# A bank for each product of a small expert, units split at most two ahead, the tail's reloads ahead of the last gate unit, and another order of its additions

## The chip, the cores and the metric

The kernel runs on one core of one Trainium2 chip. The metric is the device time of one execution in microseconds (us), the median of three runs. TensorE is called PE, ScalarE ACT, VectorE DVE, GpSimd POOL; SP issues most of the transfers (DMA).

## The reference, cut to what matters

One decoder layer over 1024 tokens of width 1024: a mixer, a mixture of 32 experts of which each token uses two, a gated addition of a per-layer input embedding (PLE), and a final norm.

```python
def expert_block(args):                      # for each expert, its rows xb
    xb, e = args
    hmid = jax.nn.silu(xb @ w1[e]) * (xb @ w3[e])
    return hmid @ w2[e]
...
h = h + hier_moe(...)                        # gates times the two experts' rows, added
e = rms_norm(p[l] @ w_ple_up[l], ple_norm[l])
gate = jax.nn.sigmoid(rms_norm(h, ple_gate_norm[l]) @ w_ple_gate[l])
h = h + gate * e
return rms_norm(h, final_norm)
```

## The kernel before

**Experts.** After routing, the experts are sorted by their number of tokens. The schedule of 32 places is `HHHHLHLHLHLHLLHLHLHLHLLHLHLHLHLL`: H is a heavy expert (up to 128 rows), L a light one (up to 64 rows; `self.light[e]`), places counted from 0. Two lights stand together at places 12 and 13, 21 and 22, and 30 and 31. Each expert has six weight units of 1 MB, two each for `w1`, `w3`, `w2`. A unit's raw copy lies in a slot (`raw`, `rawB`, `rawH`, `hb`; 13 slots in turn, so a unit's transfer waits until the unit 13 before it has let its slot go). From place 26 (`EP`) on only the six slots of `raw` and `rawB` are used. A light expert's matmuls read the raw slot itself (`W.plain`), which is free when PE has read it. A heavy expert's unit is **split** first: ACT writes the high part (L160, into `wh` or `XH`, in turn), DVE the low part (L162); the slot is free when both have read it. Each 128x512 product of a heavy expert is three matmuls (high by high, low by high, high by low; L248 to L250).

**Order.** Instructions run on each engine in the order in which this code writes them. For place `e` the loop of `moe` writes: `gemm1(e, 1)` into bank `a`; the transposes of `h` of `e-1` and their copies (`hth`, or `ht` for a light one); Silu on ACT (L1588); `gemm1(e, 3)`; the product on DVE (L1590); the transposes of the next expert's rows and their copy (`xth`, or `xt`); `gemm2(e-1)` with its result `y` and the scatter to `Y_dram`. Units are asked for in the order w1(e), w3(e), w2(e-1).

**Looking ahead.** `W.get(u, look)` writes the splits of unit `u` and of the next `look` units of heavy experts, passing over those of light ones, ahead of `u`'s matmuls:

```python
        while n < len(self.units) and (n in self.plain or look):
            look -= n not in self.plain
            n += 1
```

A split that is written early stands early in ACT's order, and what is written after it waits behind it for the unit's transfer.

**Banks.** A light expert's two products share one PSUM tile `acc`: columns 0 to 255 hold x·w1, 256 to 511 x·w3. Waits are made per tile.

**Tail.** The PLE products run as a generator (`ple`, L1201 to L1224) in half tiles of six matmuls; `fill(n)` runs n of them. `load(t)` reads tile t's two expert rows back from `Y_dram`, `tail_load(t)` the residual, `add(t)` adds them (four additions on DVE, L1798), `trans(t)` transposes the sum (L1807) and splits it into `gth`, `gtl`, `first(t)` is the first half of the gate's product, `finish` the sigmoid and what follows. There are four gate units of 1 MB.

Of the kernel before, what the change touches and what calls it, by code (L numbers as in the profile page):

```python
# [10 lines left out]
F32 = mybir.dt.float32  # L11
# [3 lines left out]
AF = mybir.ActivationFunctionType  # L15
OP = mybir.AluOpType
# [6 lines left out]
P = 128  # L23
# [12 lines left out]
NSTATIC, NLIGHT = 3, 16  # L36
HB = P // 2
# [172 lines left out]
class Layer:  # L210
# [1233 lines left out]
    def gather(self, e):  # L1444

        r, n = self.rank[e], HB if self.light[e] else P
        self.nc.gpsimd.indirect_dma_start(
            out=self.xg[e % 2][:n], out_offset=None, in_=self.g_dram,
            in_offset=bass.IndirectOffsetOnAxis(ap=self.idx_g[:n, r:r + 1], axis=0),
            bounds_check=T - 1, oob_is_err=False)  # L1450


    def moe(self):
        tc, nc, W = self.tc, self.nc, self.W
        psA, psB = self.psA, self.psB
# [7 lines left out]
        XT, HT, RX = {}, {}, {}  # L1463

        def norm_x(e):
            x = xg[e % 2]
            RX[e] = ep.tile([P, 1], F32, name="rx", bufs=3)
            if self.light[e]:
                for b in range(2):
                    nc.gpsimd.tensor_copy(RX[e][b * HB:b * HB + HB], x[:HB, D:D + 1])  # L1470
            else:
                nc.gpsimd.tensor_copy(RX[e], x[:, D:D + 1])
# [24 lines left out]
        def gemm1(e, which, acc):  # L1497
            for ui, u in enumerate(self.eu[e, which]):
                w = W.get(u, self.look(e, which))
                for kk in range(4):  # L1500
                    k = ui * 4 + kk
                    if self.light[e]:

                        o = (which == 3) * 256
                        for b in range(2):
                            self.lastmm = nc.tensor.matmul(acc[b * HB:b * HB + HB, o:o + 256], XT[e][:, k],  # L1506
                                                           w[:, kk, b * 256:b * 256 + 256],
                                                           start=k == 0, stop=k == KD - 1)
                    else:
                        th, tl = XT[e]  # L1510
                        self.mm3(acc, th[:, k], tl[:, k], w[0][:, kk], w[1][:, kk], k == 0, k == KD - 1)
                if self.light[e]:
                    W.done(u)
# [48 lines left out]
        for e in range(NE + 1):  # L1562
            last = e == NE
            if e == self.EP:
                W.split_to(self.ple_unit)
                self.ple_open()
            if not last:
                light = self.light[e]
                a = psA.tile([P, 512], F32, name="acc")
                b = a if light else psA.tile([P, 512], F32, name="acc")  # L1570
                if e + 2 < NE:
                    gather(e + 2)
                if e + 1 < NE:
                    norm_x(e + 1)
                if not e:
                    next(order)
                gemm1(e, 1, a)
                if not e:
                    next(order)
                    W.limit = 1 << 30  # L1580
            if e and e - 1 in hs:
                trans_h(e - 1, hs.pop(e - 1))
            if not last:
                h = ep.tile([P, 512], F32, name="h")
                a0 = a
                if light:
                    h, a, b = h[:, :256], a[:, :256], a[:, 256:]
                nc.scalar.activation(h, a, AF.Silu, scale=RX[e])  # L1588
                gemm1(e, 3, a0 if light else b)
                nc.vector.scalar_tensor_tensor(h, b, RX.pop(e), h, op0=OP.mult, op1=OP.mult)  # L1590
                hs[e] = h
                if not e:
                    next(order, None)
                if e + 1 < NE:
                    trans_x(e + 1)
            if e:
                gemm2(e - 1, (lambda: trans_h(e, hs.pop(e))) if e + 1 == NE else None)
                self.mark("moe %d" % (e - 1))
            if e >= 2:
                next(blocks, None)  # L1600
            if e > self.EP and not last:
                next(self.ple_gen)
# [3 lines left out]
    def look(self, e, which):  # L1606
        if which == 2 and e == NE - 1:
            return 0
        return 3


    def overflow_list(self):
# [157 lines left out]
    def tail(self):  # L1770
        tc, nc, i, W = self.tc, self.nc, self.i, self.W
        psA, psB = self.psA, self.psB
# [4 lines left out]
        def load(t):  # L1777
            if t % 2:
                y = self.rawB_pool.tile([P, 2048], F32, name="rawB", bufs=3)
            else:  # L1780
                y = self.ring.tile([P, 2048], F32, name="raw", bufs=3)
            ty[t] = (y[:, :D], y[:, D:])
            if t:
                nc.sync.dma_start(ty[t][0], self.Y_dram[t * P:(t + 1) * P])
                nc.sync.dma_start(ty[t][1], self.Y_dram[T + t * P:T + (t + 1) * P])
            else:
                for c in range(2):
                    s = slice(c * 512, c * 512 + 512)
                    nc.sync.dma_start(y.rearrange("p (k d) -> p k d", k=2)[:, :, s],  # L1789
                                      self.Y_dram.rearrange("(k t) d -> t k d", k=2)[:P, :, s])  # L1790

        def add(t):
            h = self.th[t]
            y0, y1 = ty[t]
            for c in range(2):
                for y in (y0, y1):
                    s = slice(c * 512, c * 512 + 512)
                    v.tensor_tensor(h[:, s], h[:, s], y[:, s], op=OP.add)  # L1798

        def trans(t):  # L1800
            h = self.th[t]
            th = tq.tile([P, KD, P], F32R, name="gth")
            tl = tq.tile([P, KD, P], F32R, name="gtl")
            for b in range(2):
                p = psB.tile([P, 4, P], F32, name="pb")
                for k in range(4):
                    nc.tensor.transpose(p[:, k, :], h[:, (4 * b + k) * P:(4 * b + k + 1) * P], self.ident)  # L1807
                self.split_pair(th[:, 4 * b:4 * b + 4], tl[:, 4 * b:4 * b + 4], p)
            gt[t] = (th, tl)
            st = rs[t] = tq.tile([P, 2], F32, name="tst")  # L1810
            nc.scalar.activation(ty[t][1], h, AF.Square, accum_out=st[:, 0:1])  # L1811
            self.rstd(st[:, 1:2], st[:, 0:1], D)
# [45 lines left out]
        def fill(n):  # L1858
            for _ in range(n):
                next(self.ple_gen, None)  # L1860


        W.end = None
        W.fetch_to(len(W.units))
        self.tail_load(1)
        load(0)
        load(1)
        fill(2)
        W.split_to(self.gate_units[0] + 1)
        fill(2)  # L1870
        W.split_to(self.gate_units[1] + 1)
        fill(3)
        add(0)
        fill(1)
        add(1)
        fill(1)
        self.ctxE.close()
        tq = ctxQ.enter_context(tc.tile_pool(name="tq", bufs=2, side="right", reuse_waits="tile"))
        self.fn = self.tp.tile([P, D], F32, name="tpt")
        trans(0)  # L1880
        sg = tq.tile([P, 1], F32, name="sg", bufs=1)
        nc.scalar.activation(sg, self.ones[:, 0:1], AF.Sigmoid)  # L1882
        fill(1)
        trans(1)
        fill(3)
        self.tail_load(2)
        load(2)
        nc.sync.dma_start(self.fn, bcast_rows(i["final_norm"], D))
# [3 lines left out]
        def first(t, mid=None):  # L1892
            acc = accs[t] = psA.tile([P, 512], F32, name="acc")
            gemm(t, 0, acc, mid=mid)
            finish(t, 0, acc)
# [12 lines left out]
        for t in range(NT):  # L1908
            acc = [None, None]
            if not t:  # L1910
                W.split_to(self.gate_units[2] + 1)
                first(0)
                W.ahead = 99
                W.split_to(len(W.units))
                first(1)
                add(2)
            elif t > 1:
                first(t)
            if t:
                following(t)  # L1920
            acc[1] = psA.tile([P, 512], F32, name="acc")
            if t < NT - 1:
                gemm(t, 1, acc[1])
                finish(t, 1, acc[1])
            else:
                for a, s in ((acc[1], slice(0, 256)), (psA.tile([P, 512], F32, name="acc"), slice(256, 512))):
                    gemm(t, 1, a, s)
                    finish(t, 1, a, s)
            self.mark("gate %d" % t)
            if 2 < t + 2 < NT:  # L1930
                add(t + 2)
# [52 lines left out]
```

## Time and profile before

| what | us |
|---|---|
| median of 3 runs (1308.75 to 1311.0) | 1310.31 |
| the profiled execution's own time | 1312.78 |
| its span, first to last instruction | 1311.1 |
| PE busy | 1197.2 (91%) |
| ACT busy | 581.3 (44%) |
| DVE busy | 706.3 (54%) |

Times in the trace are us from the start of the span. The experts run from about 590 to 1172, the tail from there on. "Idle before, releaser" in brackets is how long an engine stood before a row and which instruction ended that. A busy PE can run at either of two clocks; the granted clock is 1.00 at the upper one and 0.50 at the lower.

### The profile page before, as it was taken

What the parts mean: (1) busy time and instruction counts of PE and PEld (TensorE: products, weight loads), DVE (VectorE), ACT (ScalarE), POOL (GpSimd) and SP (SyncE); (2) the same over time, 40 slices, a digit from 0 to 9 for tenths busy, and PEclk for the clock granted to TensorE, in tenths of its full rate; (3) what the DMA queues carried; (4) which work ended last, traced back from release to release, by engine and by line L of the source; (5) the groups of instructions that cost most, each with busy time, mean ns of one, the idle gap of its engine ahead of it and who ended that gap; (6) DMA issues with size and microseconds to landing.
All of it is one profiled execution on the core that took longest, in us unless ns stands there. A gap on an engine that the chain in (4) does not pass through costs nothing. (4 is left out here: it accounts for less than half of the span.)

```text
span 1311.1 us, 17704 instructions
## 1 busy us (share of the span) xinstructions
PE 1197.2 (91%) x6559; PEld 932.6 (71%) x6559; DVE 706.3 (54%) x1128; ACT 581.3 (44%) x931; POOL 270.5 (21%) x378
## 2 busy tenths in 40 slices
PE   7999999999999999969999985998959987886997
PEld 7987888988888888757876663666635655544886
DVE  3557745437763545869964443454423535226665
ACT  5744343444443334227764443454423535234442
POOL 1043112305211433121211110111102101111232
PEclk9999999999999999979999997999979987898999
DMA  9323331322324356957989998999979889666421
GB/s 346 137 96 112 105 128 58 113 97 97 121 89 177 118 209 240 370 184 300 370 338 398 410 394 351 383 409 407 394 303 403 324 316 364 223 246 240 168 90 64
DMA packets 60094, 317.80 MB, mean 242 GB/s; under 512 B 9708, under 2 KB 10284, under 8 KB 30436
## 3 DMA queue, kind: packets, MB, share of 16 engines
q1 hardware_dynamic: 48196, 284.76, 56.5%
q0 software_dynamic: 11664, 31.83, 6.9%
q8 instruction: 53, 0.87, 0.3%
q14 instruction: 37, 0.30, 0.1%
q10 hardware_dynamic: 144, 0.04, 0.0%
HBM read 295.59 MB, written 29.46 MB: 248 GB/s over the span
## 5 line engine op out<-in xcount | busy, mean ns | idle before, releaser
L248 PE MATMUL acc<-wh,XH 128*128 128x512 f32 (+2 forms) x544 | 210.3, 387 | 7.6 <-ACT wh L160 6.7
L249 PE MATMUL acc<-wl,XH 128*128 128x512 f32 (+2 forms) x544 | 202.5, 372 | 1.1 <-DVE wl L162 1.1
L250 PE MATMUL acc<-wh,XL 128*128 128x512 f32 (+2 forms) x544 | 203.1, 373 | 0.3 <-DVE XL L379 0.3
L162 DVE TENSOR_TENSOR wl<-raw,wh 128x2048 fp32r<-128x2048 f32 (+4 forms) x62 | 102.7, 1672 | 82.1 <-ACT wh L160 81.8
L248 PEld LDWEIGHTS acc<-wh,XH 128*128 128x128 f32 x544 | 104.0, 191 | 23.3 <-ACT wh L160 6.9
L250 PEld LDWEIGHTS acc<-wh,XL 128*128 128x128 f32 x544 | 103.8, 191 | 17.1 <-DVE XL L379 0.5
L249 PEld LDWEIGHTS acc<-wl,XH 128*128 128x128 f32 x544 | 103.9, 191 | 16.0 <-DVE wl L162 1.6
L160 ACT ACTIVATE wh<-raw 128x2048 fp32r<-128x2048 f32 (+4 forms) x62 | 86.5, 1414 | 49.3 <-PE acc L250 28.7
L1548 POOL DMA_INDIRECT Y_dram<-y,idx_s x16 | 16.3, 1020 | 251.5 <-ACT y L1547 251.5
L1506 PE MATMUL acc<-rawH,xt 128*64 128x256 f32 x288 | 37.3, 413 | 33.5 <-ACT h L1588 30.5
L1541 POOL DMA_INDIRECT Y_dram<-y,idx_l x16 | 17.0, 1062 | 217.1 <-ACT y L1540 196.6
L162 DVE TENSOR_TENSOR XL<-raw,XH 128x1024 fp32r<-128x1024 f32 x30 | 35.3, 1219 | 48.6 <-ACT XH L160 48.6
L1590 DVE SCALAR_TENSOR_TENSOR h<-acc,rx,h 128x512 f32<-128x512 f32 (+1 forms) x32 | 19.6, 614 | 76.5 <-PE acc L1506 65.4
L1506 PEld LDWEIGHTS acc<-rawH,xt 128*64 128x64 f32 x288 | 21.6, 149 | 49.3 <-ACT h L1588 31.4
L248 PE MATMUL acc<-XH,xth 128*128 128x512 f32 x128 | 53.9, 421 | 0.3 <-ACT xth L266 0.3
L250 PE MATMUL acc<-XH,xtl 128*128 128x512 f32 x128 | 51.4, 402 | 0.3 <-DVE xtl L267 0.3
L1506 PE MATMUL acc<-raw,xt 128*64 128x256 f32 x208 | 30.3, 442 | 23.3 <-ACT h L1588 21.2
L249 PE MATMUL acc<-XL,xth 128*128 128x512 f32 x128 | 51.4, 402 | 0.0
L248 PE MATMUL acc<-XH,wh 128*128 128x512 f32 x128 | 50.9, 398 | 0.0
L248 PE MATMUL acc<-wh,xth 128*128 128x512 f32 x128 | 50.7, 396 | 0.0
L249 PE MATMUL acc<-XL,wh 128*128 128x512 f32 x128 | 50.6, 396 | 0.0
L250 PE MATMUL acc<-XH,wl 128*128 128x512 f32 x128 | 50.6, 395 | 0.0
(475 smaller groups left out, 2816.5 us busy)
## 6 DMA issues: line engine op xcount, KB each, us to landing
rawB<-in_w SPq DMA_DIRECT2D x56, 1024.0 KB, 9.9
raw<-in_w SPq DMA_DIRECT2D x53, 1024.0 KB, 11.2
rawH<-in_w SPq DMA_DIRECT2D x48, 1024.0 KB, 14.2
hb<-in_w SPq DMA_DIRECT2D x34, 1024.0 KB, 12.7
raw<-in_w_in SPq DMA_DIRECT2D x24, 1024.0 KB, 4.9
raw<-in_w_out SPq DMA_DIRECT2D x8, 1024.0 KB, 4.9
raw<-in_w_in SPq DMA_DIRECT2D x8, 768.0 KB, 6.5
xl<-in_x SPq DMA_DIRECT2D x4, 1024.0 KB, 9.5
```

The lines of the kernel that those rows point to most:

```text
L160: self.nc.scalar.activation(h[:, s], r[:, s], AF.Copy)
L162: low.tensor_tensor(l[:, s], r[:, s], h[:, s].bitcast(F32), op=OP.subtract)
L248: self.lastmm = mm(out, lh, rh, start=first, stop=False)
L249: mm(out, lh, rl, start=False, stop=False)
L250: mm(out, ll, rh, start=False, stop=last)
L1506: self.lastmm = nc.tensor.matmul(acc[b * HB:b * HB + HB, o:o + 256], XT[e][:, k], w[:, kk, b * 256:b * 256 + 256], start=k == 0, stop=k == ...
L1541: st = nc.gpsimd.indirect_dma_start(out=self.Y_dram.rearrange("t (c d) -> (t c) d", c=2), out_offset=bass.IndirectOffsetOnAxis(ap=self.idx ...
L1548: st = nc.gpsimd.indirect_dma_start(out=self.Y_dram, out_offset=bass.IndirectOffsetOnAxis(ap=self.idx_s[:, r:r + 1], axis=0), in_=y, in_of ...
L1590: nc.vector.scalar_tensor_tensor(h, b, RX.pop(e), h, op0=OP.mult, op1=OP.mult)
```

## The change

It does five things. A light expert's products get a bank each (`b` is always a tile of its own). `look` falls from 3 to 2 from place 3 on. In the tail, the rows of tiles 0 and 1 are asked for ahead of the last gate unit. The load of the sigmoid's table is written at the start of the tail. And `add(0)`, `add(1)`, `trans(1)` and the split of the third gate unit are written later among the PLE's halves: `trans(1)` now stands between the two units of `first(0)`.

```diff
-                        o = (which == 3) * 256
                         for b in range(2):
-                            self.lastmm = nc.tensor.matmul(acc[b * HB:b * HB + HB, o:o + 256], XT[e][:, k],
+                            self.lastmm = nc.tensor.matmul(acc[b * HB:b * HB + HB, :256], XT[e][:, k],
...
-                b = a if light else psA.tile([P, 512], F32, name="acc")
+                b = psA.tile([P, 512], F32, name="acc")
...
-        return 3
+        return 3 if e < NSTATIC else 2
...
+        load(0)
+        self.tail_load(1)
+        load(1)
         W.end = None
         W.fetch_to(len(W.units))
-        self.tail_load(1)
-        load(0)
-        load(1)
+        nc.scalar.activation(self.pst[:, 0:1], self.ones[:, 0:1], AF.Sigmoid)
         fill(2)
         W.split_to(self.gate_units[0] + 1)
         fill(2)
         W.split_to(self.gate_units[1] + 1)
-        fill(3)
+        fill(4)
         add(0)
-        fill(1)
-        add(1)
-        fill(1)
+        fill(2)
...
         trans(0)
-        sg = tq.tile([P, 1], F32, name="sg", bufs=1)
-        nc.scalar.activation(sg, self.ones[:, 0:1], AF.Sigmoid)
         fill(1)
-        trans(1)
-        fill(3)
+        add(1)
+        fill(2)
...
-                W.split_to(self.gate_units[2] + 1)
-                first(0)
+                first(0, lambda: trans(1))
```

On PE, the light expert at place 12 (rows of x in `xt`; its w1 product, the transposes of the heavy expert's `h`, its w3 product), before:

```order
L1506 MATMUL acc<-rawH,xt_6625 64x256 [waits DMAHW2_49,Activation_49]
L1506 MATMUL acc<-rawH,xt_6625 64x256 x7
L1506 MATMUL acc<-raw,xt_6625 64x256 [waits DMAHW3_49]
L1506 MATMUL acc<-raw,xt_6625 64x256 x7
L1729 MATMUL pb<-cst,h 128x128 [waits DVE_49]
L1729 MATMUL pb<-cst,h 128x128 x3
L1506 MATMUL acc<-rawH,xt_6625 64x256 [waits DMAHW4_49,Activation_49]
L1506 MATMUL acc<-rawH,xt_6625 64x256 x7
```

And now:

```order
L1505 MATMUL acc<-rawH,xt_6629 64x256 [waits DMAHW2_49,Activation_49]
L1505 MATMUL acc<-rawH,xt_6629 64x256 x7
L1505 MATMUL acc<-raw,xt_6629 64x256 [waits DMAHW3_49]
L1505 MATMUL acc<-raw,xt_6629 64x256 x7
L1726 MATMUL pb<-cst,h 128x128 [waits DVE_49]
L1726 MATMUL pb<-cst,h 128x128 x3
L1505 MATMUL acc<-rawH,xt_6629 64x256 [waits DMAHW4_49]
L1505 MATMUL acc<-rawH,xt_6629 64x256 x7
```

The order is the same; the first matmul of the w3 product no longer waits for ACT. The wait that is left at the first row is for the copy `xt`.

On ACT, the same place (the `y` of the light expert before, the heavy expert's `hth`, the light one's Silu into `h`, the rows `xt` of place 13, and the first two units of the heavy expert at place 14, `XH<-rawB` and `wh<-rawH`), before:

```order
L1483 ACTIVATE xt_6625<-pb 128x512
L1540 ACTIVATE y<-pb,gate_l 128x512
L160 ACTIVATE XH<-rawB 128x1024 x2
L266 ACTIVATE hth<-pb 128x512
L1588 ACTIVATE h<-acc,rx 128x256
L1483 ACTIVATE xt_6739<-pb 128x512
L160 ACTIVATE wh<-rawH 128x1024 x2
```

And now:

```order
L1483 ACTIVATE xt_6629<-pb 128x512
L1539 ACTIVATE y<-pb,gate_l 128x512
L266 ACTIVATE hth<-pb 128x512
L1585 ACTIVATE h<-acc,rx 128x256
L1483 ACTIVATE xt_6740<-pb 128x512
L160 ACTIVATE XH<-rawB 128x1024 x2
L160 ACTIVATE wh<-rawH 128x1024 x2
```

The split `XH<-rawB` moved behind `hth`, the Silu and `xt`. Every split of a heavy expert's unit from place 3 on moves back in this way by the work of one unit.

On SP, the first transfers of the tail (`xt` and `rawH` are residual tiles, `raw` and `rawB` rows of `Y_dram` or the last gate unit), before:

```order
L1768 DMA xt<-h_dram 128x1024
L120 DMA raw<-in_w_ple_gate 128x2048
L1768 DMA xt<-h_dram 128x1024
L1789 DMA raw<-Y_dram 128x2x512 x2
L1784 DMA rawB<-Y_dram 128x1024
L1785 DMA rawB<-Y_dram 128x1024
```

And now:

```order
L1765 DMA xt<-h_dram 128x1024
L1786 DMA raw<-Y_dram 128x2x512 x2
L1765 DMA xt<-h_dram 128x1024
L1781 DMA rawB<-Y_dram 128x1024
L1782 DMA rawB<-Y_dram 128x1024
L120 DMA raw<-in_w_ple_gate 128x2048
```

Tile 0's rows now stand ahead of 1.5 MB that stood before them, and the gate unit is last. SP's order among the experts is as it was.

## Rows read from the trace of the kernel before

**Rows 1.** The page's 40 slices of the span: busy share of the DMA engines, tenths.

```profile
DMA  9323331322324356957989998999979889666421
```

**Rows 2.** Windows: us, busy PE, PEld, DVE, ACT, POOL; granted clock, DMA share, GB/s.

```profile
650.00:670.00 20.00, 18.95 (x123) 13.33 (x122) 12.14 (x18) 10.53 (x14) 2.18 (x3) 1.00 0.77 297
670.00:800.00 130.00, 119.32 (x674) 81.86 (x673) 67.09 (x75) 64.41 (x84) 21.77 (x29) 0.99 1.01 403
800.00:830.00 30.00, 18.80 (x126) 12.38 (x128) 8.37 (x9) 9.26 (x13) 2.16 (x3) 0.77 0.81 318
830.00:960.00 130.00, 116.95 (x674) 78.35 (x670) 61.91 (x65) 60.25 (x79) 20.83 (x29) 0.99 1.01 404
960.00:980.00 20.00, 10.10 (x54) 6.62 (x55) 4.92 (x6) 5.91 (x8) 0.00 (x0) 0.62 0.60 233
1030.00:1110.00 80.00, 66.22 (x351) 43.54 (x350) 36.16 (x38) 35.02 (x47) 12.02 (x17) 0.88 0.86 329
1110.00:1172.00 62.00, 53.40 (x299) 32.37 (x297) 14.93 (x21) 17.97 (x34) 7.42 (x11) 0.93 0.64 233
```

**Rows 3.** Timeline of PE: start, us, line, operation, count, idle before and releaser.

```profile
729.43 1.95 PE L1506 MATMUL acc<-rawH,xt 128*64 128x256 f32 x16 [1.10 <-ACT h L1588]
...
810.47 5.81 PE L1506 MATMUL acc<-rawH,xt 128*64 128x256 f32 x32 [13.24 <-ACT h L1588]
...
969.90 3.68 PE L1506 MATMUL acc<-rawH,xt 128*64 128x256 f32 x16 [15.02 <-ACT h L1588]
...
1053.22 3.68 PE L1506 MATMUL acc<-raw,xt 128*64 128x256 f32 x16 [6.01 <-ACT h L1588]
...
1093.14 3.68 PE L1506 MATMUL acc<-raw,xt 128*64 128x256 f32 x16 [7.74 <-ACT h L1588]
...
1137.11 3.68 PE L1506 MATMUL acc<-raw,xt 128*64 128x256 f32 x16 [4.52 <-ACT h L1588]
```

**Rows 4.** Timeline of ACT around the wait at 810.

```profile
807.57 2.00 ACT L160 ACTIVATE XH<-rawB 128x1024 fp32r<-128x1024 f32 x2 [13.58 <-DMA rawB<-in_w]
809.48 0.58 ACT L266 ACTIVATE hth<-pb 128x512 fp32r<-128x512 f32 x1
```

**Rows 5.** Timeline of ACT: two splits of equal place in neighbouring pairs.

```profile
909.95 2.00 ACT L160 ACTIVATE XH<-rawB 128x1024 fp32r<-128x1024 f32 x2 [8.06 <-DMA rawB<-in_w]
...
944.98 2.00 ACT L160 ACTIVATE XH<-raw 128x1024 fp32r<-128x1024 f32 x2 [8.42 <-DMA raw<-in_w]
```

**Rows 6.** Timeline of PE and ACT before the wait at 1093, and ACT before that at 1053.

```profile
1081.19 3.62 PE L1506 MATMUL acc<-rawB,xt 128*64 128x256 f32 x32
...
1084.50 2.00 ACT L160 ACTIVATE XH<-raw 128x1024 fp32r<-128x1024 f32 x2 [6.09 <-DMA raw<-in_w]
...
1090.23 2.00 ACT L160 ACTIVATE XH<-rawB 128x1024 fp32r<-128x1024 f32 x2 [0.46 <-DMA rawB<-in_w]
...
1050.32 2.00 ACT L160 ACTIVATE XH<-rawB 128x1024 fp32r<-128x1024 f32 x2 [6.61 <-DMA rawB<-in_w]
```

**Rows 7.** Timeline of the tail's start: SP, PE, DVE and ACT.

```profile
1180.68 0.98 SPq L1789 DMA_DIRECT2D raw<-Y_dram x2
...
1184.69 1.40 DVE L1201 SCALAR_TENSOR_TENSOR rawH<-acc,pst,pn 128x512 f32<-128x512 f32 x2
...
1186.80 0.40 PE L248 MATMUL acc<-rawHh,tps 128*128 128x512 f32 x1
...
1187.97 0.40 PE L250 MATMUL acc<-rawHh,tps 128*128 128x512 f32 x1
...
1188.87 2.75 DVE L1798 TENSOR_TENSOR xt<-xt,raw 128x512 f32<-128x512 f32 x4 [2.78 <-DMA raw<-Y_dram]
...
1192.72 2.02 DVE L1798 TENSOR_TENSOR xt<-xt,rawB 128x512 f32<-128x512 f32 x3 [0.50 <-DMA rawB<-Y_dram]
...
1201.09 1.28 ACT L1882 ACT_TABLE_LOAD   x1
...
1205.77 0.76 PE L248 MATMUL acc<-XH,gth 128*128 128x512 f32 x1 [6.86 <-ACT pjunk L1222]
```

More of the change, by code (lines that the diff above doesn't have):

```diff
@@ L1584, in moe @@
                 h = ep.tile([P, 512], F32, name="h")
[L1585 to L1590, printed above, removed]
+                n = 256 if light else 512
+                nc.scalar.activation(h[:, :n], a[:, :n], AF.Silu, scale=RX[e])
+                gemm1(e, 3, b)
+                nc.vector.scalar_tensor_tensor(h[:, :n], b[:, :n], RX.pop(e), h[:, :n], op0=OP.mult, op1=OP.mult)
                 hs[e] = h
```

## The prediction

> **What bounds the kernel now.** I began with the page's slices of the span. There the DMA engines are nearly full from slice 18 on, where the experts run [rows 1], so I cut that stretch into windows. For 130 us from 670 and for 130 us from 830 their share is 1.01 at 403 and 404 GB/s [rows 2]. A pair of a heavy and a light expert (12 units of 1 MB, with gathers and scatters) costs the transfers about 35 us: the same split in neighbouring pairs waits for its DMA until 909.95 and 944.98, 35.0 us apart [rows 5]. PE needs less for the pair. In the two long windows it is busy 119.3 and 117.0 of 130 us and loses little [rows 2]. So in this stage the transfers set the pace, and a wait of PE costs time only where it makes the DMA engines stand.
>
> They do stand. The timeline of PE shows five long waits for the Silu of a light expert, 13.24, 15.02, 6.01, 7.74 and 4.52 us, and a usual one of 1.10 [rows 3]. The timeline of ACT shows why: at 807.57 a split of a unit of a later heavy expert has waited 13.58 us for its transfer, and `hth` and the Silu stand behind it in ACT's order [rows 4]. PE holds the light units' slots meanwhile. So when the late unit has landed, the transfers have filled all 13 slots and wait for PE: share 0.81 in 800 to 830, 0.60 in 960 to 980 [rows 2]. PE's clock also falls in such a wait and comes back some us later (0.77 and 0.62 there). From 1030 on only six slots serve and the share is 0.86, then 0.64 [rows 2].
>
> In the tail, the timeline shows DVE waiting for tile 0's rows until 1188.87, then for tile 1's, and PE waiting 6.86 us until the first gate matmul at 1205.77 [rows 7]. From there PE runs on to the end almost without a wait, so what that matmul gains, the kernel gains.
>
> **The change, part by part**, against the profiled execution's own 1312.8 us.
>
> *Bank and look, experts to 1030.* The bank takes away the usual 1.10 us of each light expert, but in a stage that the transfers bound this pays nothing by itself: PE then waits that much longer for a unit. What pays is that the DMA engines don't stand. I follow place 12. The split `XH<-rawB` now stands behind `hth`, Silu and `xt`. PE, which stood from 797 to 810, does the w3 product (32 matmuls, 3.6 us as in [rows 6] for w1), the heavy expert's w2 (24 matmuls at 0.23, 5.6 us, the step as in [rows 7] between 1186.80 and 1187.97), and both products of the next light expert (7.2): 16 us of work, which lets six light slots go, before it needs the `ht` that stands behind the late split. The unit lands at about 807 in either kernel, so the wait is nearly covered and the slots are free in time. I expect the share to stay at 1.0. That gives back 30 x (1 - 0.81/1.01) = 5.9 us and 20 x (1 - 0.60/1.01) = 8.1 us, 14.0 together. Against it: splits one unit later hold heavy slots one unit's work (12 matmuls, 2.8 us) longer, and around 650 to 670, where the share is 0.77 because slots are full [rows 2], this delays the transfers once. I take 2.5 for it. **Term: -11.5** (bounds 0, if the standing only moves, and -14). PE will now wait in every pair instead of at a few places, some 4 to 5 us at the copy `xt`, behind the splits of the heavy expert's w2; that is the slack between 35 and 30 us, not a loss.
>
> *Bank and look, 1030 to 1172.* Here a unit's transfer starts only when PE has used the unit six before. Before 1053, the split `XH<-rawB` waited 6.61 us ahead of `hth`, and is now behind it [rows 6]; the wait of 6.01 goes. Before 1093, the split that ends its wait at 1084.50 stays ahead of `hth`, but the one at 1090.23 (2.4 us until `hth`) leaves [rows 6], and PE passes on through the w3 product (3.6) and the transposes (0.7): of 7.74 about 1 is left. At 1137 the order of ACT is as before, and only the bank helps: 3.6 + 0.7 of 4.52. That is 6.0 + 6.7 + 4.3 = 17.0 us of waits. The transfers cap the first two: 80 x (1 - 0.86/1.01) = 11.9 us of standing in 1030 to 1110 [rows 2], and with six slots I don't expect a full share. I take half of it, 6, and 4.3 for the third. **Term: -10.5** (bounds -4.3, the part that hangs on the bank alone, and -17).
>
> *Tail.* Tile 0's rows are asked for about 1 us sooner and 1.5 MB less stands ahead of them, which at 404 GB/s [rows 2] is 3.9 us: they land at about 1184, not 1188.87. DVE is busy with the PLE until 1184.69 + 1.40 = 1186.1 [rows 7], so `add(0)` (2.75 us) starts there and ends at 1188.9. It no longer has `add(1)` (waiting until 1192.72 [rows 7]) between itself and what PE waits for. PE meanwhile runs the half at 1186.80 and the next, each six matmuls of 0.23 [rows 7], until 1189.6, then the transposes of tile 0 (1.1), then both halves of the last PLE tile (2.8): 1193.5. The bank for `first(0)` is free when DVE has finished PLE tile 6, which the table load (1.28 us, [rows 7]) and the second transposes delayed and no longer do: about 1194. So the first gate matmul moves from 1205.77 to about 1194. **Term: -12** (bounds -5 and -14). What is late next: `add(1)` runs from 1194 to 1196.7, and `trans(1)` wants it after 12 matmuls, 2.8 us after 1194, so it just holds. The third gate unit's split now stands behind the first sigmoid; `first(1)`, 24 matmuls or 5.6 us, covers its 2.6 us on ACT and 2.7 on DVE. The gate unit lands last, at about 1192, and is wanted after 1205. The table load moves to where PE waits for the rows anyway. If these covers fail, each costs 1 to 3 us.
>
> The sum: 1312.8 - 11.5 - 10.5 - 12 = 1278.8. The profiled execution is 2.5 us above the median of the runs, so for the median I say **1276**.
>
> **A rule against it.** Rows 2 give 403 and 404 GB/s over 130 us each [rows 2]. The Trainium skill, "DMA: Bandwidth & Descriptors", Specifications, states a limit of about 358 GB/s for one core's share of HBM. By it the experts' stage would already be faster than its transfers allow and nothing could be won there; the sum would be that of rival A. The measured 404 decides, and by it the standing time is real.
>
> **Rivals.**
> *A. The transfers take all of it back.* The share stays about where it is: in place of five long waits there is standing in every pair. Speaks for it: the stage is at 1.01 for 260 us, and 0.77 at 650 to 670 shows that slots can be the limit [rows 2]. Against: place 12 as followed above. Then only the tail is left: 1310.3 - 12 = 1298. It could also be that the waits move to `ht` or `hth` with the same length, which gives the same time.
> *B. More comes back.* The share is full from 670 to 1110 (14 + 11.9), the third late wait goes (4.3), with it the low clock (0.88 and 0.93 in rows 2; the first 16 matmuls after the late waits take 3.68, not 1.95 us [rows 3], and other work as long again: 3 to 4 us at each of three), and the tail gives 13: 14 + 11.9 + 4.3 + 10 + 13 = 53, so 1257.
> *C. Slower: slots.* If letting slots go later stops SP's queue at each of the 13 heavy experts after place 2, it stands 2.8 us each, 36 us; less the tail's 12 that is +24: 1334. It decides if the DMA share in 670 to 800 falls below about 0.95. Against: in a transfer-bound stage a unit is split as soon as it lands, wherever the split stands.
>
> **How the numbers follow.** My forecast 0.59, A 0.18, B 0.14, C 0.06, and 0.03 that gain and loss cancel. The terms' bounds alone give 1310.3 - 9.3 = 1301 and 1310.3 - 45 = 1265; A lies at 1298 and B at 1257. The range 1257 to 1299 leaves out C, part of B and the ends of A, about 2 in 10. A change under 0.2% (2.6 us) can't be told from none by this measurement. Faster by more: forecast, A and B, 0.91; within it 0.03; slower 0.06.
>
> **What the profile after would show.** Right: no wait of a w3 product's first matmul (L1505) for the Silu (L1585); a DMA share near 1.0 from 670 to 1030 without the holes at 800 and 960; waits of PE of some 4 to 5 us for `xt` in most pairs; place 14 begun some 6 us or more sooner in DMA terms; in the tail, tile 0's additions about 3 us sooner, and the first gate matmul about 22 us after the last expert's product, not 34. Wrong: PE waiting for `hth` or `ht` as long as it did for the Silu (A); a share under 0.95 in 670 to 800 (C); a wait of `first(0)` for its bank or of the transposes for `add(1)` (the tail's term).

## The result and the profile after

The changed kernel took 1277.42 us (median of 4 runs, 1276.12 to 1280.49) and the kernel before, beside it, 1309.88: a ratio of 0.976 (0.974 to 0.978). The profiled execution had a span of 1278.8 us, 32.3 less than that of before. 1276 was forecast.

The windows of the kernel after, cut as in [rows 2] as far as they go (us, busy time of PE, PEld, DVE, ACT and POOL, granted clock, DMA share, GB/s):

```profile
650.00:670.00 20.00, 20.00 (x132) 14.40 (x131) 14.93 (x21) 12.74 (x17) 2.82 (x3) 1.00 0.78 288
670.00:800.00 130.00, 122.34 (x680) 83.25 (x680) 66.89 (x75) 64.65 (x85) 24.53 (x29) 0.96 1.02 403
800.00:830.00 30.00, 30.00 (x187) 20.05 (x184) 12.01 (x14) 12.60 (x18) 6.05 (x7) 1.00 1.02 405
830.00:960.00 130.00, 116.65 (x651) 77.00 (x650) 58.49 (x61) 57.09 (x75) 20.62 (x25) 0.93 1.00 398
960.00:980.00 20.00, 20.00 (x127) 12.67 (x126) 6.69 (x8) 7.14 (x11) 2.17 (x3) 1.00 1.02 409
1040.00:1110.00 70.00, 67.23 (x357) 45.55 (x357) 31.69 (x35) 34.16 (x49) 11.07 (x14) 0.95 0.93 367
1110.00:1146.00 36.00, 30.08 (x160) 16.25 (x155) 8.79 (x14) 9.81 (x20) 4.83 (x9) 0.86 0.75 287
```

Both holes of [rows 2] are gone: 318 became 405 GB/s in 800 to 830 and 233 became 409 in 960 to 980. Against 650 to 670 (297 to 288) and 830 to 960 (404 to 398) that leaves 2.6 + 3.5 - 0.2 - 0.8 = 5.1 MB more moved, 12.7 us at 404 GB/s.

The waits of PE from 600 to 1215, one line of the kernel before and two of the kernel after, and the timeline of PE at four places that answer to [rows 3] and [rows 6]:

```profile
PE acc L1506 <- ACT h L1588: 57.5, 16, 15.0
...
PE acc L1505 <- ACT xt L1483: 27.9, 8, 6.0
PE pb L1527 <- ACT ht L1494: 4.6, 1, 4.6
```

```profile
842.66 3.68 PE L1505 MATMUL acc<-hb,xt 128*64 128x256 f32 x16 [6.04 <-ACT xt L1483]
...
912.25 5.36 PE L1505 MATMUL acc<-rawH,xt 128*64 128x256 f32 x32 [2.50 <-ACT xt L1483]
...
947.06 3.25 PE L1505 MATMUL acc<-rawH,xt 128*64 128x256 f32 x14 [2.77 <-ACT xt L1483]
...
1072.64 0.50 PE L248 MATMUL pb<-XH,hth 128*128 128x512 f32 x1 [1.93 <-ACT hth L266]
```

No matmul waits for a Silu any more; the 57.5 us of such waits before have become 27.9 us of waits for `xt`. There are eight, about one in a pair, and those at 912 and 947 stand 34.8 us apart, the pace that two splits had in [rows 5]. So PE still waits for the transfers, but they go on meanwhile. In the longest of these waits the share is 1.01:

```profile
836.60:842.66 6.06, 0.02 (x3) 0.00 (x1) 3.81 (x4) 4.55 (x6) 0.00 (x0) 0.89 1.01 422
```

ACT at place 12, which answers to [rows 4]:

```profile
798.98 0.47 ACT L1585 ACTIVATE h<-acc,rx 128x256 f32<-128x256 f32 x1
802.74 0.60 ACT L1483 ACTIVATE xt<-pb 128x512 f32<-128x512 f32 x1 [3.29 <-PE pb L1482]
808.04 2.01 ACT L160 ACTIVATE XH<-rawB 128x1024 fp32r<-128x1024 f32 x2 [4.70 <-DMA rawB<-in_w]
```

The late unit lands when it did (808.04, before 807.57), but the Silu starts at 798.98, ahead of it.

The tail's start, which answers to [rows 7] (SP, ACT, PE and DVE):

```profile
1151.24 0.89 SPq L1786 DMA_DIRECT2D raw<-Y_dram  x2
...
1158.22 0.47 PE L248 MATMUL acc<-rawHh,tps 128*128 128x512 f32 x1 [2.52 <-DVE te L1201]
...
1160.30 2.74 DVE L1795 TENSOR_TENSOR xt<-xt,raw 128x512 f32<-128x512 f32 x4
...
1165.43 1.03 PE L1804 MATMUL pb<-cst,xt 128*128 128x128 f32 x8
...
1168.86 0.40 PE L250 MATMUL acc<-rawHh,tps 128*128 128x512 f32 x1
...
1169.29 1.08 ACT L266 ACTIVATE gth<-pb 128x512 fp32r<-128x512 f32 x2 [2.92 <-PE acc L250]
...
1172.01 0.47 PE L248 MATMUL acc<-XH,gth 128*128 128x512 f32 x1 [2.76 <-ACT pjunk L1222]
```

Tile 0's additions wait for no transfer now. But `gth`, the copy of tile 0's transposes, waits 2.92 us, not for these (done at 1166.5), but for the last matmul of the PLE.

For all kernels (the experiments follow below), times are cut at four marks of the trace: the Silu of place 0 (597.64 before, 597.02 after), that of place 25 (1033.12 and 1020.26), the last expert's `y` (1171.97 and 1146.01), the first gate matmul (1205.77 and 1172.01), and the span's end.

| kernel | median us | place 0 to 25 | to last `y` | to first gate matmul | to the end |
|---|---|---|---|---|---|
| before | 1309.88 | 435.48 | 138.85 | 33.80 | 105.3 |
| after | 1277.42 | 423.24 | 125.75 | 26.00 | 106.8 |
| bank alone | 1288.58 | 426.09 | 127.08 | 32.44 | 104.4 |
| look alone | 1291.05 | 422.94 | 132.94 | 32.38 | 105.1 |
| bank and look | 1280.67 | 425.48 | 122.23 | 32.20 | 104.9 |
| tail alone | 1304.43 | 435.30 | 137.78 | 26.02 | 106.7 |
| after, light `y` apart | 1277.46 | 423.08 | 123.14 | 26.00 | 106.7 |
| after, `gth` free | 1273.08 | 423.53 | 122.61 | 22.99 | 105.1 |
| after, one unit ahead | 1271.57 | 420.75 | 121.95 | 25.99 | 106.8 |
| after, two products | 1273.41 | 420.19 | 124.97 | 25.78 | 106.5 |
| after, `gth` free, one ahead | 1268.21 | 421.71 | 120.63 | 23.09 | 105.0 |
| after, `gth` free, none ahead | 1376.64 | 506.97 | 144.63 | 22.27 | 105.1 |
| after, again | 1276.44 | 423.44 | 122.61 | 25.96 | 106.8 |

The last row is another execution of the same kernel: its stretch up to the last `y` is 3.1 us shorter than in the first, so a difference of that size in one profile of that column says nothing. The kernels ran in four groups, each beside the kernel before (medians 1308.4 to 1310.3), so a difference between two kernels of different groups is good to some 2 us; the bank, the look, both and the tail alone are one group, the last row and the two above it another. One of the ten runs of the tail alone took 1514.71 us, at a granted clock of 0.74 where the others had 0.96 or 0.97; without it the median is 1304.10.

### The profile page after: what moved, and what is told of

The parts are those of the page before. It is cut to its first block, busy times and chain, and to the rows that moved or that the text cites. A ratio compares the mean times of both kernels' runs of the same rounds, so it can differ in the third digit from the quotient of the medians.

```text
span 1278.8 us, 17687 instructions
## 1 busy us (share of the span) xinstructions
PE 1202.0 (94%) x6559; PEld 933.8 (73%) x6559; DVE 705.5 (55%) x1128; ACT 579.6 (45%) x931; POOL 280.2 (22%) x378
## 5 line engine op out<-in xcount | busy, mean ns | idle before, releaser
L162 DVE TENSOR_TENSOR XL<-raw,XH 128x1024 fp32r<-128x1024 f32 x30 | 35.4, 1221 | 66.5 <-ACT XH L160 66.4
L250 PE MATMUL acc<-wh,xtl 128*128 128x512 f32 x128 | 50.6, 395 | 0.0
L249 PE MATMUL acc<-wl,xth 128*128 128x512 f32 x128 | 50.5, 394 | 0.0
L160 ACT ACTIVATE XH<-raw 128x1024 fp32r<-128x1024 f32 x30 | 30.0, 1050 | 43.6 <-DMA raw<-in_w 43.6
```

What stands on the lines that cost most here:

```text
L160: self.nc.scalar.activation(h[:, s], r[:, s], AF.Copy)
L162: low.tensor_tensor(l[:, s], r[:, s], h[:, s].bitcast(F32), op=OP.subtract)
L249: mm(out, lh, rl, start=False, stop=False)
L250: mm(out, ll, rh, start=False, stop=last)
```

## The experiments

### One part alone, or two

The bank alone (the kernel before with `b` always a tile of its own and the columns that belong to it, as in the change's first hunks):

```diff
-                b = a if light else psA.tile([P, 512], F32, name="acc")
+                b = psA.tile([P, 512], F32, name="acc")
```

> The kernel before with a bank for each product of a light expert, and nothing else. Theory (the transfers pace the experts to 1030, and a late split still stands ahead of hth and the Silu): the usual 1.1 us at each light expert goes but is waited elsewhere, and in the five long waits PE gets the 3.6 us of the w3 product done and then stops for hth. About -10 us against before (1300; bounds -5 and -14). Rival (PE paces the stage, every wait for a Silu is worth its length): -30 us or more, since it takes away all waits for the Silu. Place 24's Silu: theory 4 to 8 us earlier.

Measured: 1288.58 us, a ratio of 0.984 (0.981 to 0.986), -21.7 us, twice what I expected and short of the rival. The timeline of PE at place 12 shows what I had got wrong:

```profile
796.02 3.67 PE L1505 MATMUL acc<-rawH,xt 128*64 128x256 f32 x32
799.63 0.71 PE L1482 MATMUL pb<-cst,xt 64*128 64x64 f32 x8
807.76 0.80 PE L248 MATMUL pb<-XH,hth 128*128 128x512 f32 x1 [7.42 <-ACT hth L266]
```

PE still waits, 7.42 us for `hth` in place of 13.24 for the Silu [rows 3]. But the 32 matmuls ahead of the wait have let two light slots go, and SP asks for the next units in them at 798 and 800, where it did at 814 and 816 before. On SP, the waits from 798 to 815 for PE to be done with a light unit, before and with the bank alone:

```profile
SPq L120 <- PE acc L1506: 16.4, 1, 16.4
...
SPq L120 <- PE acc L1505: 2.5, 2, 1.4
```

That alone fills over half of either hole: 365 GB/s in 800 to 830, 327 in 960 to 980.

```profile
800.00:830.00 30.00, 22.24 (x132) 13.90 (x131) 10.44 (x13) 12.40 (x18) 3.18 (x4) 0.89 0.95 365
...
960.00:980.00 20.00, 15.27 (x93) 10.14 (x93) 8.27 (x9) 9.26 (x13) 2.16 (x3) 0.83 0.82 327
```

Two units ahead alone:

```diff
-        return 3
+        return 3 if e < NSTATIC else 2
```

> The kernel before with splits at most two units ahead from place 3 on, and nothing else. Theory: the late split leaves hth and the Silu, the long waits of 13 and 15 us fall to a few us, the usual 1.1 us at each light expert stays; the DMA share stays near 1.0 through 800 and 960. About -16 us (1294; bounds -10 and -22). Rival 1 (the bank does it all): within 2 us of before. Rival 2 (slots that are let go later stop the transfers): slower than before, DMA share under 0.95 in 670 to 800.

Measured: 1291.05 us, 0.985 (0.982 to 0.988), -19.2 us. As the theory had it, some of the waits for the Silu are left, and the share is full through both holes:

```profile
PE acc L1506 <- ACT h L1588: 28.9, 16, 7.5
```

```profile
800.00:830.00 30.00, 29.23 (x189) 19.22 (x186) 12.01 (x14) 12.72 (x18) 6.06 (x7) 1.00 1.01 401
...
960.00:980.00 20.00, 16.50 (x105) 9.22 (x104) 6.69 (x8) 6.78 (x10) 2.17 (x3) 0.91 1.01 394
```

Both rivals fall (the share in 670 to 800 is 1.02). In the table, the look takes all that the change takes up to place 25 (-12.5 us) and 5.9 behind it; the bank takes 9.4 and 11.8.

Both, with the old tail:

> Bank and two units ahead, with the tail of before. Theory: -26 us (1284), the 26.0 us by which the last expert's product moved between the two traces; the two parts overlap in the holes of the DMA share, so less than the sum of each alone is no surprise. Rival (the new tail also gives time to the experts, or the other way round): not within 2 us of the kernel after plus 6.

Measured: 1280.67 us, 0.977 (0.974 to 0.980), -29.6 us; the stretch from place 0 to the last `y` is 26.6 us shorter, as expected. Each alone has 21.2 and 18.5 there, 39.7 together, 13 us more than both. 12 of these 13 lie before place 25, where the two holes are that either fills. The sign that was set for the rival (not within 2 us of 1283.4) came by the median, by under 1 us; the interval, 1276 to 1284 us, leaves it open. The traces speak for a small part of it: the stretch behind the last `y` is 137.1 us, 2.0 less than before with the same tail.

The new tail alone:

```diff
+        load(0)
+        self.tail_load(1)
+        load(1)
         W.end = None
         W.fetch_to(len(W.units))
-        self.tail_load(1)
-        load(0)
-        load(1)
...
-                first(0)
+                first(0, lambda: trans(1))
```

> The kernel before with the new tail only: reloads ahead of the last gate unit, table load early, other order of the additions. Theory: -6 us (1304), as the traces show of the stretch from the last expert's product on (first gate matmul 7.8 us earlier after it, the rest 1.5 us longer). Rival: -12, the term of the prediction, if the low clock after the last expert and the waits at 1158 hang on the faster experts.

Measured: 1304.43 us, 0.996 (0.994 to 0.998), -5.8 us; 7.8 us less to the first gate matmul, 1.4 more behind it. So the rival, the prediction's -12, is refuted. The gains of the two parts don't quite add: 29.6 + 5.8 = 35.4, and the whole change gave 32.5. In the traces, the faster experts already take 2.0 us from the stretch behind the last `y` (the row of bank and look), and the new tail takes 4.3 more from it there, 6.4 where it stands alone.

### Do the transfers set the pace?

The third product of the heavy experts at places 3 to 25 is left out:

```diff
         mm(out, lh, rl, start=False, stop=two and last)
+        if two:
+            return
         mm(out, ll, rh, start=False, stop=last)
```

> The changed kernel without the third product (low rows by high weights) of the heavy experts at places 3 to 25; this changes what is computed. That is 24 of 72 matmuls of 0.23 us for each of these 12 experts, 5.6 us each. Theory (transfers pace places 4 to 25): a pair still takes about 35 us, place 24 comes at most 6 us sooner and the whole is 1270 to 1277. Rival (PE paces): 67 us less, about 1210.

Measured: 1273.41 us, 0.972 (0.970 to 0.975), 4.0 us less than the changed kernel, from another group. (There are eleven heavy experts in these places, not twelve, so 62 us of matmuls were left out.) The rival is refuted. The windows of this kernel and of the changed one over the whole stage:

```profile
670.00:1010.00 340.00, 271.35 (x1558) 166.77 (x1558) 156.17 (x172) 152.94 (x206) 59.31 (x71) 0.90 1.01 401
```

```profile
670.00:1010.00 340.00, 312.79 (x1775) 207.56 (x1774) 156.61 (x172) 154.13 (x206) 59.43 (x71) 0.95 1.01 402
```

PE's 41 us less of work in it don't raise the rate. They turn into waiting for `xt`, where the changed kernel has 27.9 us:

```profile
PE acc L1507 <- ACT xt L1485: 70.4, 9, 10.1
```

A light expert's `y` in memory of its own:

```diff
-            y = ep.tile([P, D], F32, name="y", tag="y" if e < NE - 1 else "xth")
+            yl = light and e < self.EP
+            y = ep.tile([P, 512 if yl else D], F32, name="y", tag="tps" if yl else "y" if e < NE - 1 else "xth")
```

> The changed kernel, with the result of a light expert at places below 26 in a tile of its own, so that it no longer waits until the heavy expert's result has been scattered. Theory (transfers pace the stage): the two waits of ACT for that scatter (4.96 and 7.35 us) and PE's wait of 6.8 us at the pair of lights go, and PE waits as much longer at the next copy xt, so the time moves by 0 to -2 us (1276). Rival (PE's waits are worth their length): -7 to -12 us.

Measured: 1277.46 us, 0.976 (0.974 to 0.978), the changed kernel's own time. The wait for the scatter had been this one, in the timeline of ACT of the changed kernel:

```profile
822.65 0.69 ACT L1539 ACTIVATE y<-pb,gate_l 128x512 f32<-128x512 f32 x1 [4.96 <-DMA Y_dram<-y,idx_s]
```

Both such waits go, and the waits of PE for `xt` rise from 27.9 to 32.9 us. In a stage that the transfers bound, a wait that goes comes back as another, and its length says nothing of what it is worth.

### How far ahead

One unit ahead from place 3 on:

```diff
-        return 3 if e < NSTATIC else 2
+        return 3 if e < NSTATIC else 1
```

> The changed kernel with splits at most one unit ahead from place 3 on. Theory: the late splits that are left ahead of hth and ht leave too, but PE now waits for the low part of the next unit (2.7 us of DVE for each unit against 2.8 us of matmuls), at most 1 us a unit; transfers still pace to 1010, so within 5 us of the changed kernel (1272 to 1282). Rival (slots that are let go later stop the transfers): DMA share under 0.95 in 670 to 800 and 1300 or more.

Measured: 1271.57 us, 0.972 (0.970 to 0.974), 5.9 us less than the changed kernel (the two are of different groups; the run of both edits, below, says how much of it holds), a little past the edge that I gave; the rival is refuted (share 1.02 in 670 to 800). The waits of PE (total us, times, longest us) have these three among them:

```profile
PE acc L1505 <- ACT xt L1483: 13.8, 5, 4.0
PE acc L248 <- ACT wh L160: 4.4, 2, 2.5
...
PE pb L249 <- DVE wl L162: 1.9, 11, 0.2
```

The waits for a unit's split are few and mostly 0.2 us, and those for `xt` are halved.

With the free `gth` of the next section as well, no unit ahead at all:

```diff
-        return 3 if e < NSTATIC else 2
+        return 3 if e < NSTATIC else 0
```

> As the kernel with both edits, but a heavy expert's unit is split only when it is asked for itself (look 0 from place 3 on). Theory: PE now waits for ACT and DVE at each heavy unit, about 1 to 2 us (the first part of the high split, 1.0 us, and the low one behind it), at 13 experts of six units: 80 to 150 us of waits, of which the transfers hide some 5 us a pair; so slower than with one unit ahead by 20 to 60 us (1290 to 1330). Rival (the transfers hide all of it): within 3 us of the kernel with one unit ahead.

Measured: 1376.64 us, 1.052 (1.050 to 1.054), 108 us slower than one unit ahead. The direction is the theory's, the size not: I had let the transfers hide 5 us in a pair. PE's waits for a split come to 93 us (41.8 + 22.4 + 17.2 + 11.7), inside the 80 to 150 expected, and the loss is no smaller than they are. Over the stage:

```profile
670.00:1010.00 340.00, 282.72 (x1418) 188.02 (x1415) 132.37 (x144) 129.29 (x170) 47.74 (x57) 0.90 0.88 331
```

331 GB/s in place of 402: a raw slot is free only when its unit is split, and here the split waits for PE, so the transfers stand as well. One or two units ahead lie between the two ways to lose.

### The missed wait in the tail

The left operand of the last PLE tile lies in memory over which `gth` of tile 0 is put; the pool makes `gth` wait for that operand's last reader. Here it lies elsewhere:

```diff
-                                  tag="xtl" if t in (3, 5, 7) else "tps"))
+                                  tag="y" if t == 7 else "xtl" if t in (3, 5) else "tps"))
```

> The changed kernel, with the left operand of the last PLE tile in other memory, so that gth of tile 0 waits for its four transposes alone and no longer for the last PLE matmul. Theory (that wait is what the tail's term missed): gth at about 1166.3 instead of 1169.3 in terms of the changed kernel's trace, the first gate matmul right behind the last PLE matmul (wait of 2.8 us down to under 0.5), -2.5 us (1275). Rival (the finish of PLE tile 6, behind the rows and the gate unit's split, sets it): the wait stays over 2 us and the time is the same.

Measured: 1273.08 us, 0.973 (0.971 to 0.975), 4.3 us less than the changed kernel (the two intervals overlap a little; the traces settle it: from the last `y` to the end 128.1 us, where the six other kernels with the new tail and without the free `gth` have 132.3 to 132.8 in the table). Its timeline:

```profile
1162.04 1.04 PE L1804 MATMUL pb<-cst,xt 128*128 128x128 f32 x8
...
1162.88 1.08 ACT L266 ACTIVATE gth<-pb 128x512 fp32r<-128x512 f32 x2
...
1165.72 0.39 PE L248 MATMUL acc<-XH,gth 128*128 128x512 f32 x1
```

`gth` follows its transposes, and the first gate matmul starts without a wait. It comes 3.0 us sooner after the last `y`, and 1.7 us more are saved behind it: the changed kernel, after its wait, runs at the lower clock, this one at the upper. The window behind the first gate matmul, of the changed kernel and of this one:

```profile
1172.00:1175.50 3.50, 3.49 (x9) 2.78 (x10) 3.43 (x6) 0.69 (x2) 2.21 (x4) 0.55 1.04 369
```

```profile
1165.70:1169.20 3.50, 3.50 (x20) 2.92 (x20) 2.99 (x5) 0.75 (x3) 2.45 (x4) 1.00 0.69 238
```

Granted clock 0.55 against 1.00, 9 matmuls against 20 in the same 3.5 us.

Both edits that gained, and the changed kernel again beside it:

> The changed kernel with one unit ahead from place 3 on and the left operand of the last PLE tile in other memory: the two edits that gained alone. Theory (one is in the experts, 6 us, the other behind them, 4.5 us, with nothing in common): the gains add, 1267 (1265 to 1269). Rival (the low clock at the first gate matmul is all that the second edit saves, and comes back): 1270 to 1272.

> The changed kernel once more, on the same chip as the two others. Every theory: 1277 (1275 to 1280), a ratio of 0.976 to before.

Measured: 1268.21 us, 0.969 (0.967 to 0.971), against 1276.44 us, 0.974 (0.972 to 0.976). The gain is 8.2 us by the medians and 6.8 by the means, and the two intervals are apart; it is less than the sum of the two alone, 10.2, which were taken against a changed kernel of another group. The traces say where it lies: 3.7 us up to the last `y` and 4.7 behind it. The tail's part is the same as alone. One unit ahead is worth less than the 5.9 us, and no more than the noise of that column: that it is no slower than two is safe, how much faster it is stays open. The rival is refuted: the first gate matmul comes 23.1 us after the last `y`, without the wait, and the end 105.0 us after it. This kernel has the lowest median of all; its interval overlaps those of either edit alone.

## Why the prediction was right, and where not

**What bounds the stage** was right, and is shown: 62 us of matmuls taken away gave 3 us up to place 25.

**First term, to 1030: -11.5, measured -12.9** (the Silu of place 25, at 1033.12, came at 1020.26; 0.6 of it stood at place 0 already). The route was as followed: the late split stands behind the Silu, the share stays at 1.0, and the 5.1 MB more are worth 12.7 us. The holes gave slightly more than 14.0, and the loss at 650 to 670 was 0.2 MB, 0.4 us, not 2.5; 0.8 MB, 2 us, were lost in 830 to 960, where the term had nothing. What I had not seen is that the look alone fills the holes and the bank alone over half of them.

**Second term, 1030 to 1172: -10.5, measured -13.1** (16.2 in the column of the second profile). The step that was mis-sized is "the part that hangs on the bank alone", -4.3, at the third wait only. With the bank alone the three late waits of 6.01, 7.74 and 4.52 us [rows 3] have become these, all from its timeline of PE:

```profile
1043.58 0.50 PE L248 MATMUL pb<-XH,hth 128*128 128x512 f32 x1 [0.16 <-ACT hth L266]
...
1078.90 0.80 PE L248 MATMUL pb<-XH,hth 128*128 128x512 f32 x1 [3.81 <-ACT hth L266]
...
1118.70 0.50 PE L250 MATMUL pb<-XH,htl 128*128 128x512 f32 x1 [0.83 <-DVE htl L267]
```

It gains 11.8 us in that stretch, twice the look's 5.9. Where only six slots serve, two slots let go ahead of the wait are a third of them; that this is why the bank counts for more here is an argument, no run took it apart. At the last light expert a wait that the term did not count grew: `ht` stands behind the split of the first gate unit, which waits for its transfer, and PE waits 4.63 us for it, 3.27 before. The 16 matmuls behind it then run at the lower clock (granted 0.57; before 1.00) and take 6.34 us, not 3.65. PE before, ACT and PE after:

```profile
1168.27 3.65 PE L1528 MATMUL pb<-rawB,ht 128*64 128x512 f32 x16 [3.27 <-ACT ht L1494]
...
1136.85 2.56 ACT L151 ACTIVATE XH<-rawB,cols 128x512 fp32r<-128x512 f32 x4 [10.23 <-DMA rawB<-in_w_ple_gate]
...
1139.62 6.34 PE L1527 MATMUL pb<-rawB,ht 128*64 128x512 f32 x16 [4.63 <-ACT ht L1494]
```

**Tail: -12, measured -6.3** (7.8 us to the first gate matmul, 1.5 lost behind it). The rows did come in time: `add(0)` starts 14.3 us after the last `y`, before 16.9. Two steps failed. "PE meanwhile runs ... until 1189.6, then the transposes of tile 0": they came 19.4 us after the last `y`, not 17.6, since PE waits 2.52 us for a PLE finish (`te`) that stands behind the split of the second gate unit (`wl`) on DVE, and then runs at the lower clock. Most of the 1.8 us is the clock: the kernel before has this wait too, 1.88 us, but then a granted clock of 1.00 (1183.90 to 1187.90), and the four halves behind it take 1.5 us longer now. It comes with the new tail and not with the faster experts, as the tail alone has the transposes 19.4 us after its last `y` too; why the clock falls here and did not before stays open. The timeline of DVE and a window of the changed kernel:

```profile
1156.33 0.74 DVE L152 SCALAR_TENSOR_TENSOR wl<-rawB,cols,wh 128x512 fp32r<-128x512 f32 x1
...
1157.33 1.40 DVE L1201 SCALAR_TENSOR_TENSOR te<-acc,pst,pn 128x512 f32<-128x512 f32 x2
```

```profile
1158.00:1162.00 4.00, 3.78 (x10) 3.04 (x11) 3.96 (x8) 0.73 (x3) 0.74 (x3) 0.59 1.04 428
```

And "the bank for `first(0)` is free ... about 1194" left out that `gth` waits for the last PLE matmul. The trace of before had it, in a row that the prediction does not use:

```profile
1198.95 1.08 ACT L266 ACTIVATE gth<-pb 128x512 fp32r<-128x512 f32 x2 [9.80 <-PE acc L250]
```

The transposes of tile 0 were done by 1192.9 there. Taking this wait away gave 3.0 + 1.7 of the 5.7 us that the term was short of; the 1 us that is left fits the wait at 1158 and its clock, which was not tried by itself. Of the 1.5 us lost behind the first gate matmul, 1.4 are two waits that the kernel before does not have, at the transposes of tile 2 (0.65 and 0.74 us, the second for its additions on DVE); the prediction had the additions of tiles 0 and 1 only. (The lower clock behind that matmul is no part of this loss: the kernel before has it there too.)

The sum of the terms was 34.0 us and 32.3 came, since the experts gave 1.4 and 2.6 us more and the tail 5.7 less: part of the hit is luck.

**The rivals.** A (waits move and the transfers stand as before) is refuted: waits moved to `xt`, but the transfers go on in them. B came true in half: 32.3 us of its 53. C is refuted for two units ahead and for one (share 1.02 in 670 to 800), and comes true with none ahead (0.89). The rule by the Trainium skill's "DMA: Bandwidth & Descriptors", Specifications (about 358 GB/s for a core's share of HBM) does not bind this kernel: 402 GB/s stood for 340 us on end, and the stage got faster.

## What to carry to other kernels

In a stage that transfers bound, price an edit by the bytes that move in the windows where the DMA share falls, not by the length of the waits it removes; an edit that lets slots go ahead of a wait can fill a hole too (here over half of it), as one that removes the wait does, and the two don't add. Splitting ahead costs when a late unit's split stands in front of short work that others need, so try the smallest distance that still keeps the slots turning (here one or two; none cost 108 us). Where a pool is laid over a closed one, read what the first writer of each tile waits for: the releaser's name in the timeline (here a matmul that the copy doesn't read) shows it.

## What was not expected of the hardware

With the holes filled, each transfer took longer to land: from issue to landing, 1 MB into `rawH` took a median 14.8 us in 670 to 800 before and 17.3 after (`raw` 17.4 and 18.5, `rawB` 18.5 and 21.7), at the same 403 GB/s. This fits more units under way together that share the rate; no run took it apart. The landing of a single unit (839.77 before, 837.63 after, read where a split waited for it) showed only 2 us of a gain that the bytes put at 6 by then.
